# The same fp32 two-block transformer kernel, with its instructions ordered by the framework's finer simulation

## The chip, the cores and the metric

The kernel runs on one core of one Trainium2 chip. The metric is device time in microseconds (us) from launch to end, lower is better. A core has a matrix engine (TensorE, PE in the rows; PEld is its weight load), a vector engine (DVE), an activation engine (ScalarE, ACT), GpSimd (POOL) and SyncE (SP), which here only issues transfers. Each engine runs its own list of instructions in the order in which the program holds them and waits on semaphores for the others.

## The reference

One sequence of 256 tokens, width 1024, all in fp32. First two layers of a mixer with a gate behind it, then one conditioned block with a convolution, a pooling branch and a gated feed-forward:

```python
for i in range(2):                                    # first block
    h = rms_norm(x, pre_norm_g[i])
    y = retention_branch(h, ...) if i == 0 else mla_branch(h, ...)
    x = x + rms_norm(y, post_norm_g[i])
    x = x + (p[i] @ ple_w_proj[i]) * sigmoid(x @ ple_w_gate[i])
mod = silu(c) @ w_ada + b_ada                         # second block
sh1, sc1, g1, sh2, sc2, g2 = split(mod, 6)
h = layer_norm(x) * (1 + sc1) + sh1
# conv branch, pooling branch, two sigmoid gates, all from h @ w_in
mix = (sigmoid(gate_a) * (silu(layer_norm(conv)) @ w_pw) + sigmoid(gate_b) * yb) @ w_out
x = layer_norm(ALPHA * x + g1 * mix)
h = layer_norm(x) * (1 + sc2) + sh2
v, gt = split(causal_dwconv(h @ w_up), 2)
x = layer_norm(ALPHA * x + g2 * ((gelu(gt) * v) @ w_down))
```

The retention branch has 4 heads in two chunks of 128 tokens. The latent attention (MLA) has 16 heads with a causal softmax.

## The kernel before

Activations are kept transposed, 128 features on the partitions and 256 tokens along the row; a `Blk` holds 4 such blocks per tile (named half_N). To be exact in fp32, most products are made from three passes: every operand is split into a high part and a low rest, and `mm` (L232 to L234) issues high times high, high times low and low times high. `mm32` (L238) is the plain fp32 product. The moving side of a pass is 256 columns in most places.

Weights (in_wts) stream in pieces of 128x1024 through SP: `fetch` (L163) loads raw_N, `load` then makes wh_N on ACT (L176) and wl_N on DVE (L177); 6 raw, 5 wh and 5 wl buffers turn round. Activations are split the same way by `split`: ACT writes the high part (L185), DVE the low part (L186):

```python
A.copy(hi, raw)
V.tensor_sub(lo, raw, hi.bitcast(F32))
```

Beside this stream runs the conditioning product `silu(c) @ w_ada`: 48 chunks adach_N of 128x1024, each loaded by SP (L401, two buffers) and reduced on DVE (L408). They are spread through the first two layers by a rate (`mod_rate`).

The order has two makers. The trace of the Python code fixes the order in which instructions are made: `after(us, fn)` and `tick` keep a clock of matmul time and call a prepared step, such as the softmax of a head, when its due time has come. The framework then orders each engine's instructions again before they are fixed, with a simulation of the engines that says which instruction is ready when. The loads of the conditioning chunks (L401) are held in program order among themselves, the rest is free within its data dependences and its buffers.

Sums over features, as the norms need them, are made on PE by a product with a matrix of ones: L336 (`put`) adds one block into a PSUM bank, and the norm can be read only when the last block has been added. L358 does it for a head of the retention. `rms_neg2` and `newton` (L374, L376, L362, L365, L368) make the norm factor from the bank, `ln_stats` the same for a layer norm (L382 to L388).

Four places are spoken of later. `post` ends a layer of the first block:

```python
for k, n in ((0, 1), (1, 1), (2, 2), (4, 2), (6, 1), (7, 1)):
    V.tensor_mul(x1.span(k, n), x1.span(k, n), bc2(nry, n))      # L679
    V.tensor_add(x1.span(k, n), x1.span(k, n), x.span(k, n))     # L680
    split(x1p[0].span(k, n), x1p[1].span(k, n), x1.span(k, n))   # L185, L186
```

and `half_outer` then starts the product with `ple_gate` from the first of these blocks. PE works meanwhile on `ple_proj` (php_N, its result copied by ACT at L724). In the MLA, `mla_scores` makes for each head a row maximum (L874, L875, L877), the exponential on ACT (L879, L880) and the division on DVE (L882, L887), and `mla_turn` transposes the result on PE (L898). `lora` norms the latent (L774, L777, L780, then L185, L186). `modulate` makes the input of the feed-forward (L962, L963, ACT L967, DVE L970 and L974). Behind the convolution, L1162 and a split make the input of `w_pw`.

## Time and profile before

| | |
|---|---|
| time, median of 3 runs | 851.39 us (851.32 to 853.29) |
| the profiled execution: time and span | 853.2 us, 851.4 us |
| PE busy | 834.8 us, 98% of the span |
| DVE busy | 713.2 us, 84% |
| ACT busy | 550.6 us, 65% |
| POOL busy | 9.7 us, 1% |
| weights and other reads from memory | 165.41 MB, 196 GB/s over the span |
| granted TensorE clock, mean | 0.997 |

The span reaches from the first to the last instruction of the core; 1.8 us of the profiled execution lie around it. Busy time of PE is modelled from pipelined matmuls, so that matmuls which follow closely overlap in their rows: the spacing of their starts is what one costs. Times in rows are us from the start of the span.

### The profile page before, as it was taken

The page shows a single profiled execution, that of the slowest core. Times are in us where ns is not written, and L with a number is a line of the kernel's source. Part 1 is how long each engine was busy: PE and PEld are TensorE (multiplying, and loading weights), DVE is VectorE, ACT ScalarE, POOL GpSimd, SP SyncE. Part 2 cuts the span into 40 slices and gives each one's busy share as a digit, 9 for nine tenths or more (in the row PEclk, how much of TensorE's full clock was granted, in tenths as well). Part 3 has the DMA queues.
Part 4 walks back from the last instruction along what each step waited for, and adds up shares of the span by engine and source line. Part 5 has one row for each costly group of instructions (what it writes and reads, how often), then busy time and mean ns, then how long its engine had stood idle before and what let it go on. Part 6 is the DMA issues. An engine that isn't in the chain of part 4 may idle for free.

```text
span 851.4 us, 15952 instructions
## 1 busy us (share of the span) xinstructions
PE 834.8 (98%) x6218; PEld 798.2 (94%) x6218; DVE 713.2 (84%) x1287; ACT 550.6 (65%) x928; POOL 9.7 (1%) x28
## 2 busy tenths in 40 slices
PE   8999999999999999999999999999999999999995
PEld 6989899999999999999999998999999999999885
DVE  6999787898889978699874677899687888889996
ACT  6656555545676686787653757999756576666550
POOL 0000000000000000000000000000000000000001
PEclk9999999999999999999999999999999999999998
DMA  9866566678557647365355354245463365567722
GB/s 334 321 233 235 204 211 245 243 254 293 188 173 243 242 150 237 136 243 179 118 168 174 142 205 156 85 174 177 146 226 134 136 194 179 194 205 253 275 86 74
DMA packets 46634, 167.48 MB, mean 197 GB/s; under 512 B 5216, under 2 KB 5472, under 8 KB 46560
## 3 DMA queue, kind: packets, MB, share of 16 engines
q1 hardware_dynamic: 45936, 164.38, 55.0%
q0 software_dynamic: 624, 2.10, 0.9%
q8 instruction: 48, 0.79, 0.4%
q14 instruction: 26, 0.21, 0.1%
HBM read 165.41 MB, written 1.05 MB: 196 GB/s over the span
## 4 chain that ended last, share of the span: by engine, by line
PE 93%; DVE 4%; DMA 1%; ACT 1%; issue 1%; DVEq 0%; SPq 0%; ACTq 0%
PE ps L233 27%; PE ps L232 26%; PE ps L234 26%; PE ps L238 10%; PE ps L336 1%; PE ps L358 1%; DVE wl L177 1%; PE ps L898 1%; DMA adach<-in_wada 1%; DMA raw<-in_wts 1%; DVE half L679 0%; ACT wh L176 0%; DVE half L680 0%; PE ps L1146 0%; DVE t L1410 0%
## 5 line engine op out<-in xcount | busy, mean ns | idle before, releaser
L232 PE MATMUL ps<-half,wh 128*128 128x256 f32 x1504 | 424.8, 283 | 1.4 <-ACT half L185 1.4
L233 PE MATMUL ps<-half,wh 128*128 128x256 f32 x1504 | 423.6, 282 | 0.6 <-DVE half L186 0.5
L234 PE MATMUL ps<-half,wl 128*128 128x256 f32 x1504 | 422.1, 281 | 0.3 <-DVE wl L177 0.3
L176 ACT CAST wh<-raw 128x1024 fp32r<-128x1024 f32 x233 | 242.9, 1048 | 147.7 <-PE ps L233 94.3
L177 DVE TENSOR_TENSOR wl<-raw,wh 128x1024 fp32r<-128x1024 f32 x233 | 282.3, 1219 | 58.3 <-ACT wh L176 55.8
L233 PEld LDWEIGHTS ps<-half,wh 128*128 128x128 f32 x1504 | 283.3, 188 | 1.9 <-DVE half L186 0.9
L232 PEld LDWEIGHTS ps<-half,wh 128*128 128x128 f32 x1504 | 282.4, 188 | 2.6 <-ACT half L185 2.0
L234 PEld LDWEIGHTS ps<-half,wl 128*128 128x128 f32 x1504 | 283.9, 189 | 0.6 <-DVE wl L177 0.5
L238 PE MATMUL ps<-half,raw 128*128 128x256 f32 (+2 forms) x384 | 84.9, 380 | 0.0
L238 PEld LDWEIGHTS ps<-half,raw 128*128 128x128 f32 x384 | 72.5, 190 | 10.0
L232 PE MATMUL ps<-wh,half 128*128 128x512 f32 (+1 forms) x202 | 72.7, 361 | 0.0
L234 PE MATMUL ps<-wh,half 128*128 128x512 f32 (+1 forms) x202 | 71.0, 351 | 0.0
L233 PE MATMUL ps<-wl,half 128*128 128x512 f32 (+1 forms) x202 | 71.0, 351 | 0.0
L408 DVE CUSTOM_DVE_ANT_0 adach<-adach,siluc 128x1024 f32<-128x1024 f32 x48 | 58.3, 1218 | 11.5 <-DMA adach<-in_wada 11.5
L1063 ACT ACTIVATE t<-apad,vec 128x256 f32<-128x256 f32 x106 | 44.3, 500 | 0.5 <-DVE half L1064 0.5
L233 PEld LDWEIGHTS ps<-wl,half 128*128 128x128 f32 x202 | 38.1, 189 | 5.5 <-DVE wl L177 0.4
L232 PEld LDWEIGHTS ps<-wh,half 128*128 128x128 f32 x202 | 38.0, 188 | 5.5 <-ACT wh L176 0.2
L234 PEld LDWEIGHTS ps<-wh,half 128*128 128x128 f32 x202 | 38.0, 188 | 5.5
L1064 DVE TENSOR_TENSOR half<-half,t 128x512 f32<-128x512 f32 x53 | 36.4, 687 | 3.7 <-ACT t L1063 1.8
L185 ACT CAST half<-t 128x256 fp32r<-128x256 f32 (+1 forms) x47 | 20.3, 452 | 16.9 <-DVE t L1323 10.9
L186 DVE TENSOR_TENSOR half<-t,half 128x256 fp32r<-128x256 f32 (+1 forms) x47 | 21.7, 483 | 3.6 <-ACT half L185 2.7
L1318 ACT ACTIVATE t<-ps,vec 128x256 f32<-128x256 f32 x38 | 21.0, 558 | 2.0 <-PE ps L234 1.2
(277 smaller groups left out, 971.1 us busy)
## 6 DMA issues: line engine op xcount, KB each, us to landing
raw<-in_wts SPq DMA_DIRECT2D x257, 512.0 KB, 4.3
adach<-in_wada SPq DMA_DIRECT2D x48, 512.0 KB, 5.1
half<-in_xT SPq DMA_DIRECT2D x4, 256.0 KB, 6.9
half<-in_rows POOLq DMA_DIRECT2D x2, 512.0 KB, 5.2
out<-t SPq DMA_DIRECT2D x4, 256.0 KB, 2.0
cst<-in_cst SPq DMA_DIRECT2D x1, 928.0 KB, 10.1
raw<-in_wts SPq DMA_DIRECT2D x2, 256.0 KB, 5.1
siluc<-in_cv SPq DMA_DIRECT2D x1, 512.0 KB, 8.1
```

Of the source, the lines that this page charges most:

```text
L176: A.copy(hi, raw)
L177: V.tensor_sub(lo, raw, hi.bitcast(F32))
L185: A.copy(hi, src)
L186: V.tensor_sub(lo, src, hi.bitcast(F32))
L232: T.matmul(ps, l[0], r[0], start=first, stop=False)
L233: T.matmul(ps, l[0], r[1], start=False, stop=False)
L234: T.matmul(ps, l[1], r[0], start=False, stop=last)
L238: T.matmul(ps, w, r, start=first, stop=last)
L408: V.tensor_tensor_reduce(ch, ch, sc, 1.0, 0.0, MUL, ADD, mod[:, n:n + 1])
L1063: A.activation(t[:, b, :], apad[:, i0 + b, k:k + S], AF.Copy, scale=w[b])
L1064: V.tensor_add(acc.pair(i0 // 2), acc.pair(i0 // 2), t)
L1318: A.activation(t[:, b, :], ps[:, b, :], AF.Identity, bias=col("b_dw_f_2", m), scale=w[2])
```

## The change

The context in which the kernel is built is told to order the instructions with the framework's finer simulation of the engines (a timeline) in place of its default one. The kernel's body is the same:

```diff
-    with tile.TileContext(nc) as tc:
+    with tile.TileContext(nc, schedule_with_timeline_sim=True) as tc:
         tile_kernel(tc, order, *aps, out)
```

Both programs hold the same instructions on the same tiles, but for one more table load on ACT; the order on PE, DVE, ACT and SP differs from the start of layer 0 to the end. Three places show how.

**DVE, in `post` of layer 0**, between the norm factor and the first low parts. t1_417 is the norm factor nry, half_413 and half_414 are x1, half_1 and half_2 are x, half_434 is the low part of x1 and wl_451 and wl_457 are low parts of weights that are used later. Before:

```order
L365 TENSOR_TENSOR t1_419_2520<-t1_415_2513,t1_418_2518 128x256
L368 SCALAR_TENSOR_TENSOR t1_417_2517<-t1_419_2520,t1_416_2515 128x256
L679 TENSOR_TENSOR half_413_2508<-half_413_2508,t1_417_2517 128x256 x2
L680 TENSOR_TENSOR half_413_2508<-half_413_2508,half_1_75 128x256 x2
L679 TENSOR_TENSOR half_413_2508<-half_413_2508,t1_417_2517 128x512
L679 TENSOR_TENSOR half_414_2509<-half_414_2509,t1_417_2517 128x512
L680 TENSOR_TENSOR half_413_2508<-half_413_2508,half_1_75 128x512
L186 TENSOR_TENSOR half_434_2600<-half_413_2508,half_432_2598 128x256 x2
```

And now:

```order
L365 TENSOR_TENSOR t1_419_2520<-t1_415_2513,t1_418_2518 128x256
L177 TENSOR_TENSOR wl_451_2723<-raw_449_2720,wh_450_2722 128x1024
L368 SCALAR_TENSOR_TENSOR t1_417_2517<-t1_419_2520,t1_416_2515 128x256
L679 TENSOR_TENSOR half_413_2508<-half_413_2508,t1_417_2517 128x256 x2
L679 TENSOR_TENSOR half_413_2508<-half_413_2508,t1_417_2517 128x512
L679 TENSOR_TENSOR half_414_2509<-half_414_2509,t1_417_2517 128x512
L679 TENSOR_TENSOR half_414_2509<-half_414_2509,t1_417_2517 128x256 x2
L680 TENSOR_TENSOR half_413_2508<-half_413_2508,half_1_75 128x256
L177 TENSOR_TENSOR wl_457_2762<-raw_455_2759,wh_456_2761 128x1024
L680 TENSOR_TENSOR half_413_2508<-half_413_2508,half_1_75 128x256
L680 TENSOR_TENSOR half_413_2508<-half_413_2508,half_1_75 128x512
L680 TENSOR_TENSOR half_414_2509<-half_414_2509,half_2_76 128x512
```

Behind these come two more L680 and then the first L186. All six products L679 and all six sums L680 now stand ahead of the first low part, and two weight pieces among them.

**PE, at the start of the same `post`**: ps_409 is the bank of the norm's sums, t2_412 the last block that goes into it, ps_428 and ps_429 belong to `ple_proj`. Before:

```order
L336 MATMUL ps_409_2485<-t2_411_2502,ones_98 128x256
L232 MATMUL ps_428_2542<-php_391_2363,wh_421_2530 128x256
L233 MATMUL ps_428_2542<-php_392_2364,wh_421_2530 128x256
L336 MATMUL ps_409_2485<-t2_412_2505,ones_98 128x256
L234 MATMUL ps_428_2542<-php_391_2363,wl_422_2531 128x256
```

And now, twelve matmuls of ps_428 and five of ps_429 later than ps_409's other blocks:

```order
L232 MATMUL ps_429_2556<-php_391_2363,wh_421_2530 128x256
L233 MATMUL ps_429_2556<-php_392_2364,wh_421_2530 128x256
L336 MATMUL ps_409_2485<-t2_412_2505,ones_98 128x256
L234 MATMUL ps_429_2556<-php_391_2363,wl_422_2531 128x256
L232 MATMUL ps_429_2556<-php_391_2363,wh_421_2530 128x256
```

The matmul that closes the bank has moved from behind 2 matmuls of `ple_proj` to behind 17.

**DVE, in the MLA near 398 us**: sm_858 is the softmax tile of one head, sm_860 its negated maximum, sm_862 one over its sum. Before:

```order
L877 TENSOR_SCALAR sm_860_4930<-sm_859_4927 128x2
L943 TENSOR_SCALAR ms_6471<-s1_6470 128x8
L1203 TENSOR_TENSOR gs_7666<-s1_6470,vec_77 128x8
L177 TENSOR_TENSOR wl_908_5172<-raw_906_5169,wh_907_5171 128x1024
L882 RECIPROCAL sm_862_4935<-sm_861_4932 128x2
L887 TENSOR_SCALAR sm_858_4926<-sm_858_4926,sm_862_4935 128x128
```

And now:

```order
L177 TENSOR_TENSOR wl_914_5201<-raw_912_5198,wh_913_5200 128x1024
L877 TENSOR_SCALAR sm_860_4930<-sm_859_4927 128x2
L186 TENSOR_TENSOR t2_872_5004<-ps_870_4990,t2_871_5003 128x512
L177 TENSOR_TENSOR wl_920_5224<-raw_918_5221,wh_919_5223 128x1024
L177 TENSOR_TENSOR wl_926_5253<-raw_924_5250,wh_925_5252 128x1024
L747 TENSOR_TENSOR t1_889_5072<-ps_876_5024,cos4_122 128x256
L748 TENSOR_TENSOR t1_888_5067<-t1_888_5067,sin4_123 128x256
L186 TENSOR_TENSOR al_882_5051<-ps_880_5046,ah_881_5050 128x384
L882 RECIPROCAL sm_862_4935<-sm_861_4932 128x2
L749 TENSOR_TENSOR t1_889_5072<-t1_889_5072,t1_888_5067 128x256
L887 TENSOR_SCALAR sm_858_4926<-sm_858_4926,sm_862_4935 128x128
```

The head's last steps now stand behind three later weight pieces (wl_914, wl_920, wl_926) and the turn of the head before it; further up, a reduce of the conditioning product (adach_996) and two splits (t2_869, half_545) have also come ahead of them.

## Rows read from the trace of the kernel before

**Rows 1.** Page, part 1: busy time and share of the span.

```profile
span 851.4 us, 15952 instructions
...
PE 834.8 (98%) x6218; PEld 798.2 (94%) x6218; DVE 713.2 (84%) x1287; ACT 550.6 (65%) x928; POOL 9.7 (1%) x28
```

**Rows 2.** Page, part 4: chain that ended last, shares by engine.

```profile
PE 93%; DVE 4%; DMA 1%; ACT 1%; issue 1%; DVEq 0%; SPq 0%; ACTq 0%
```

**Rows 3.** Waits of PE: total us, times, longest us.

```profile
PE ps L336 <- DVE t L326: 2.5, 1, 2.5
```

**Rows 4.** Page, part 5: busy us, mean ns of one, idle ahead, its releaser.

```profile
L177 DVE TENSOR_TENSOR wl<-raw,wh 128x1024 fp32r<-128x1024 f32 x233 | 282.3, 1219 | 58.3 <-ACT wh L176 55.8
L408 DVE CUSTOM_DVE_ANT_0 adach<-adach,siluc 128x1024 f32<-128x1024 f32 x48 | 58.3, 1218 | 11.5 <-DMA adach<-in_wada 11.5
```

**Rows 5.** Timeline of PE, 215 to 222 us: start, duration, instruction.

```profile
215.43 0.59 PE L336 MATMUL ps<-t,ones 128*128 128x256 f32 x2
...
217.30 0.28 PE L234 MATMUL ps<-php,wl 128*128 128x256 f32 x1
217.41 0.28 PE L232 MATMUL ps<-php,wh 128*128 128x256 f32 x1
...
222.04 0.38 PE L233 MATMUL ps<-half,wh 128*128 128x256 f32 x1 [0.26 <-DVE half L186]
```

**Rows 6.** Timeline of DVE, 216 to 222 us; in brackets idle time ahead, its releaser.

```profile
216.06 0.42 DVE L374 TENSOR_SCALAR t<-ps 128x256 f32<-128x256 f32 x1 [1.25 <-PE ps L336]
...
217.95 0.42 DVE L368 SCALAR_TENSOR_TENSOR t<-t,t 128x256 f32<-128x256 f32 x1
218.41 0.76 DVE L679 TENSOR_TENSOR half<-half,t 128x256 f32<-128x256 f32 x2
219.09 0.76 DVE L680 TENSOR_TENSOR half<-half,half 128x256 f32<-128x256 f32 x2
219.76 1.28 DVE L679 TENSOR_TENSOR half<-half,t 128x512 f32<-128x512 f32 x2
...
221.56 0.75 DVE L186 TENSOR_TENSOR half<-half,half 128x256 fp32r<-128x256 f32 x2
```

**Rows 7.** Timeline of PE and DVE, 481 to 487 us.

```profile
481.53 0.59 PE L336 MATMUL ps<-t,ones 128*128 128x256 f32 x2
...
486.46 0.75 DVE L186 TENSOR_TENSOR half<-half,half 128x256 fp32r<-128x256 f32 x2
...
486.93 0.38 PE L233 MATMUL ps<-half,wh 128*128 128x256 f32 x1 [0.28 <-DVE half L186]
```

**Rows 8.** Timeline of DVE and PE, 387 to 400 us.

```profile
387.15 1.23 DVE L177 TENSOR_TENSOR wl<-raw,wh 128x1024 fp32r<-128x1024 f32 x1 [1.61 <-ACT wh L176]
...
397.98 0.55 DVE L887 TENSOR_SCALAR sm<-sm,sm 128x128 f32<-128x128 f32 x2
...
399.64 0.82 PE L898 MATMUL ps<-ident,sm 128*128 128x128 f32 x6
```

**Rows 9.** Timeline, three other starts of a product: 284, 611 and 671 us.

```profile
284.62 0.62 PE L232 MATMUL ps<-half,wh 128*128 128x256 f32 x3 [1.37 <-ACT half L185]
...
612.15 1.28 ACT L1186 ACT_TABLE_LOAD   x1
...
662.27 0.59 PE L336 MATMUL ps<-t,ones 128*128 128x256 f32 x2
...
671.21 0.75 DVE L974 TENSOR_TENSOR half<-t,half 128x256 fp32r<-128x256 f32 x2
```

**Rows 10.** Stretches: busy us of PE, PEld, DVE, ACT, POOL (instructions), granted clock, DMA share, GB/s.

```profile
24.00:60.00 36.00, 36.00 (x263) 33.98 (x262) 35.70 (x66) 21.56 (x27) 0.00 (x0) 1.00 0.72 275
206.00:213.00 7.00, 5.33 (x46) 5.12 (x44) 7.00 (x9) 6.01 (x11) 0.00 (x0) 1.00 0.80 280
842.00:844.00 2.00, 0.73 (x7) 0.53 (x5) 1.99 (x6) 0.20 (x1) 1.69 (x1) 1.00 0.00 0
846.00:848.00 2.00, 0.00 (x0) 0.00 (x0) 1.93 (x5) 0.00 (x0) 0.00 (x0) 0.71 0.35 131
848.00:850.00 2.00, 0.00 (x0) 0.00 (x0) 0.26 (x1) 0.00 (x0) 0.00 (x0) 0.50 0.70 262
```

## The prediction

> **What bounds the kernel now.** I read the shares of the span first: PE is busy for 834.8 of 851.4 us, DVE for 84% of them and ACT for 65% [rows 1]. The chain that ended last lies on PE for 93% and on DVE for 4% [rows 2]. So PE's list of matmuls is the bound, and another order can change the time only by the stalls in it. I then went through the starts of PE's matmuls. Two that follow each other without a stall are 0.11 to 0.12 us apart (217.30 and 217.41 [rows 5]); what lies above that comes to about 19 us in the whole span, most of it the 5 us of the first loads and two waits, 2.5 us for the sums of a norm (L326) [rows 3] and 1.37 us for the first half of the MLA's latent (L185) [rows 9]. A better order can win 10 to 15 us at most, since the first loads stay.
>
> Next I read how near PE already is to a wait. At the start of `ple_gate0` the first low part L186 starts at 221.56; two of them take 0.75, so the first ends near 221.98, and the matmul that reads it starts at 222.04 [rows 5, 6]. At `ple_gate1` the distance is as small: L186 starts at 486.46, its matmul at 486.93 [rows 7]. Whatever is put ahead of these instructions on DVE comes on to PE at once. DVE isn't free to take it up either: its busy time is 35.70 of 36.00 us in the stretch from 24 to 60 us and 7.00 of 7.00 from 206 to 213 us [rows 10]. Lastly I compared the two orders with these rows.
>
> **What the change does, place by place.** It adds and removes no work but a table load. What moves has a pattern: DVE takes a weight's low part (L177) or a conditioning reduce (L408) that is ready ahead of the step of a serial chain (norm, softmax, split) that isn't, and takes all pieces of one kind before the next kind; PE gets the matmul that closes a sum later. Weight pieces and reduces are dear: 1.22 us each in the group's mean [rows 4], about 1.13 when they follow each other. Where PE waits for the chain, the moved pieces are the price.
>
> *post, layer 0 (222 us).* Before, DVE does L368, two L679, two L680, two long L679, one long L680, then the first L186. From 217.95, the start of L368, to the end of that L186 this takes 4.0 us [rows 6]. Now ahead of L186 stand besides the same pieces two more short L679 (0.76 for a pair that overlaps, 0.67 net), one long L680 (0.6, half of the long pair's 1.28) and two more short L680 (0.67), and two weight pieces (2 x 1.13): 4.2 us. On PE the closing L336 moves from behind 2 matmuls of `ple_proj` to behind 17; 15 matmuls at 0.118 are 1.77, and as the first five of the bank's six matmuls still stand first it lands near 217.0 in place of 215.43 [rows 5]: 1.6 us. Together 5.8; of later stalls of 0.2 and 0.4 us some are taken up, so I put down **5.2**. Below, 3.5 if the norm chain has slack for the closing matmul; above, 6.
>
> *post, layer 1 (486 us).* The same six L679 and six L680 (2.56 us each kind) now stand whole ahead of L186, where two L679, two L680 and one long L679 stood (1.95): 3.2 more, and two weight pieces, 2.3. The closing L336, at 481.53 before [rows 7], moves by 4 matmuls, 0.5. Sum 6.0, less the same absorbed stalls: **5.3**, between 4.6 and 6.
>
> *MLA, one head (398 us).* Before, the two L887 end near 398.5 and the transposes L898 of their tile start at 399.96, within the six that the row at 399.64 groups, so 1.7 us of slack for the first L887, which starts at 397.98 and takes 0.28 [rows 8]. Now ahead of them stand one reduce, three weight pieces, three splits of 512 columns (0.6 each) and L747, L748, L749 and one split of 384 columns (1.5 together): 1.14 + 3.4 + 1.8 + 1.5 = 7.8 us. DVE idles 1.61 us at 387 for a weight's high part [rows 8]; a reduce moves in there, which saves 1.2. PE's own list ahead of the transposes grows by 0.35. 7.8 - 1.2 - 1.7 - 0.35 gives **4.5**, between 3.5 and 5.7 (without the saving).
>
> *Latent of q (284 us).* PE already waits 1.37 us [rows 9]. A reduce and a weight piece (2 x 1.14) and a 512-column step (0.6) come ahead of L780, while another reduce and a weight piece leave the place just before it: **2.5**, between 1 and 2.9.
>
> *Start of w_pw (611 us).* ACT does all four L1162 before the first L185 (1.1 later), and the table load, 1.28 [rows 9], an activation (0.6) and a weight's high part (1.05) before the second; a weight's low part stands ahead of the second L186. PE's filling matmuls cover a part: 1.1 + 0.9 + 0.5 gives **2.3** net, between 0.7 and 3.
>
> *Start of w_up (671 us).* The closing L336 at 662.27 [rows 9] moves behind five fp32 matmuls of 0.44 and its sum's others, to near 666.2. Followed step by step (two norm chains, a copy on ACT ahead of L388, four L963 of 0.6, a weight piece of 1.13, four L970 of 0.33 in a row) the first L974 starts at about 675.3 in place of 671.21 [rows 9]: **4.0**, between 2 and 4.2.
>
> *Layer 0 to 213 us.* Reduces are drawn ahead of the heads' chains; by the moved pieces up to 2.6 us at 60 us, where DVE is full, 1.9 at 137 and 5.6 over 158 to 200. By hand 5. But the 2.5 us wait at 211 [rows 3] is one in which DVE is full [rows 10] because it had waited for conditioning chunks (11.5 us in the whole span [rows 4]). A PE that comes later waits less there, so I take off 2.5: **2.5**, between 0 and 7.6. The loads of those chunks move up on SP by a place or a few; the bytes are the same.
>
> *The rest.* Nine smaller places have bounds of 0.2 to 1.9, and after PE's end the stores of the first half come later by some 0.5: **1.2** in all, between 0 and 6.
>
> Sum: 5.2 + 5.3 + 4.5 + 2.5 + 2.3 + 4.0 + 2.5 + 1.2 = 27.5 us. The profiled execution took 853.2, of which 1.8 lie around the span; its span of 851.4 equals the median of the timed runs, so I add to that: **879 us**, 3.2% slower.
>
> **One thing the sum leaves out.** PE's last matmul ends at 842.73 (0.73 us of work in the stretch from 842) and nothing follows; the granted clock is still 1.00 then, 0.71 on average from 846 to 848 and 0.50 behind [rows 10], so it fell from 2.4 to 1.2 GHz after about 4.1 us without a matmul. The longest wait inside the span, 2.5 us, left it at 1.00 [rows 3, 10]. The waits that I forecast at 222, 486 and perhaps 398 and 671 us are 4 to 6 us long. The Trainium skill (TensorE: Matmul & The Clock Gate, part 1, on the clock gate) states that the clock goes back to the lower level when the engine has been idle and comes back only after sustained work; the trace's end agrees with the fall, and no run here shows the return.
>
> **The rivals.**
> 1. *Slower, and the clock falls too.* Four waits over 4.1 us. If each were followed by as long a stretch at half speed as it took to fall, an estimate from the 4.1 us above, it would cost 2 us each: 27.5 + 8, about 887. For it speaks the end of the trace; against it, that two of the four waits are only just so long, and that a return sooner than assumed would cost less. Chance 25%.
> 2. *Slower by half.* DVE is idle for 16% of the span, and a step that I take for late has been drawn up somewhere earlier: every place comes to its lower end, 3.5 + 4.6 + 3.5 + 1 + 0.7 + 2 is 15.3, 867 us. Chance 18%.
> 3. *No change.* The moved pieces are needed soon anyway, and the waits become earlier ones of the same length. That holds only where PE has slack at the moved step. Against it stands the 0.06 us between L186 and its matmul at 222 and the likeness of 486 [rows 5 to 7]. 851, chance 4%.
> 4. *Faster.* The order draws weight pieces ahead so far that PE's waits on weights, splits and the conditioning chunks at 211 and 284 vanish: 2.5 + 1.4 and some 4 of the small ones, 843 us. It would decide if the pieces ahead of L186 at 222 and 486 were done before the norm factor was ready; at 222 DVE's longest idle there is 1.25 us [rows 6], room for one piece of 1.22 and not for two. Chance 5%.
>
> The forecast of 879 has the remaining 48%, with 872 to 884 as its own range. The range that leaves out no more than 2 in 10 reaches from the lower ends to the fallen clock: 862 to 895. A difference under 0.3% (2.6 us) can't be told from none. Slower by more 91%, within 4%, faster 5%.
>
> **What would show it.** In the profile after, PE should wait about 6 us at `ple_gate0` and `ple_gate1`, released by L186, with two L177 among DVE's rows ahead of it; about 4.5 us at an L898, released by L887; about 4 us at the first L974 of `w_up`; and the 2.5 us at L326 should be smaller. PE's busy time should hardly change while the span grows. I would be wrong in the pieces if those waits are under 2 us, and wrong in all if the sum of PE's waits in the span isn't some 25 us larger. A granted clock below 1.00 behind those waits would speak for the first rival.

## The result: 938 us, 10% slower

The changed kernel takes 938.17 us (median of four runs, 930.26 to 938.93), the kernel before 852.34 beside it. The ratio is 1.097, with a 95% interval of 1.094 to 1.101. The forecast had the sign and the mechanism; the time lies 59 us above it, and outside the range. Three runs of the experiments that took over a third longer than the others of their kernel (1193, 1383 and 1673 us) are left out of every time below.

The page of the changed kernel, parts 1, 4 and 5; they answer to [rows 1, 2, 4]:

```profile
span 936.7 us, 15978 instructions
...
PE 860.4 (92%) x6218; PEld 818.6 (87%) x6218; DVE 718.1 (77%) x1287; ACT 552.8 (59%) x929; POOL 10.2 (1%) x28
...
PE 72%; DVE 14%; DMA 8%; ACT 3%; issue 2%; SPq 0%; DVEq 0%; ACTq 0%
...
L177 DVE TENSOR_TENSOR wl<-raw,wh 128x1024 fp32r<-128x1024 f32 x233 | 283.9, 1221 | 96.6 <-ACT wh L176 95.6
...
L408 DVE CUSTOM_DVE_ANT_0 adach<-adach,siluc 128x1024 f32<-128x1024 f32 x48 | 58.6, 1222 | 27.1 <-DMA adach<-in_wada 27.1
```

DVE and ACT have the same work as before, within 5 us. PE's busy time grew by 26 us with the same 6218 matmuls: they took longer, at a lower clock. The chain that ended last left PE for a fifth of the span more than before and went to DVE and to the transfers of the conditioning chunks. DVE's idle time ahead of weight pieces went from 58 to 97 us, ahead of reduces from 11.5 to 27: an instruction that isn't ready now stands first more often.

The waits of PE in the changed kernel (total us, times, longest us); before, the longest was the one of [rows 3]:

```profile
PE ps L232 <- ACT half L185: 14.5, 4, 5.2
PE ps L358 <- DVE t L297: 12.3, 4, 5.6
PE ps L898 <- DVE sm L887: 9.1, 3, 5.4
PE ps L232 <- ACT half L967: 7.4, 2, 5.5
PE ps L233 <- DVE half L186: 5.3, 3, 2.2
PE ps L1146 <- DVE half L1064: 3.0, 1, 3.0
PE ps L232 <- ACT t L185: 2.8, 1, 2.8
PE ps L233 <- DVE half L974: 2.3, 1, 2.3
```

The spacing of matmul starts gives the account. For each matmul I took the distance to the next one, less the median distance of the same kind in the kernel before; what is left is called excess. Excess over 0.3 us at full clock is a wait: 66.8 us now, 7.1 before. Excess where the granted clock is below 0.99 is the clock: 22.5 us now, none before. The smaller excess went from 10.3 to 7.3. The last matmul starts 13.5 us before the end of the span in place of 8.9. That is 59.7 + 22.5 - 3.0 + 4.6 = 83.8 of the 85.3 us between the two spans; the rest isn't assigned.

Where PE waits (the places with a wait of 1.9 us or more now or before, each place's sum), by the same spacing:

| place, us of the changed kernel | released by | us | forecast, net |
|---|---|---|---|
| heads of layer 0: 44, 64, 147, 201 | L185, then L297 | 3.0 + 4.0 + 5.8 + 2.1 | 2.5 with the next line |
| sums of layer 0: 232 | L326 | 0.3, was 2.7 | in the line above |
| `post`, layer 0: 240, 244 | L185, L186 | 6.0 | 5.2 |
| latent of q: 310 | L185 | 5.4, was 1.5 | 2.5 |
| MLA, two transposes: 433, 436 | L887 | 8.7 | 4.5 |
| `post`, layer 1: 530, 534 | L185, L186 | 6.0 | 5.3 |
| first layer norm: 580, 588 | L967 | 6.1 | in "the rest" |
| convolution: 633 | L1064 | 3.2 | in "the rest" |
| start of `w_pw`: 677, 693 | L185, L186 | 3.7 | 2.3 |
| `w_up`: 717, 734, 746, 749 | L345, L326, L967, L974 | 6.7 | 4.0 |

The end of layer 0 is the case that the prediction worked out at most length. The timeline of DVE in the changed kernel (start, duration, instruction):

```profile
236.27 0.42 DVE L374 TENSOR_SCALAR t<-ps 128x256 f32<-128x256 f32 x1 [1.93 <-PE ps L336]
...
238.18 1.23 DVE L177 TENSOR_TENSOR wl<-raw,wh 128x1024 fp32r<-128x1024 f32 x1
239.32 0.42 DVE L368 SCALAR_TENSOR_TENSOR t<-t,t 128x256 f32<-128x256 f32 x1
239.77 2.63 DVE L679 TENSOR_TENSOR half<-half,t 128x256 f32<-128x256 f32 x6
242.32 0.42 DVE L680 TENSOR_TENSOR half<-half,half 128x256 f32<-128x256 f32 x1
242.66 1.22 DVE L177 TENSOR_TENSOR wl<-raw,wh 128x1024 fp32r<-128x1024 f32 x1
243.80 2.29 DVE L680 TENSOR_TENSOR half<-half,half 128x256 f32<-128x256 f32 x5
246.01 2.29 DVE L186 TENSOR_TENSOR half<-half,half 128x256 fp32r<-128x256 f32 x5
```

And that of PE there, with what follows the wait:

```profile
239.60 0.28 PE L234 MATMUL ps<-php,wl 128*128 128x256 f32 x1
243.29 1.01 PE L232 MATMUL ps<-half,wh 128*128 128x256 f32 x3 [3.41 <-ACT half L185]
246.47 0.58 PE L233 MATMUL ps<-half,wh 128*128 128x256 f32 x1 [2.17 <-DVE half L186]
246.85 0.42 PE L234 MATMUL ps<-half,wl 128*128 128x256 f32 x1
```

From L368 to the end of the first L186 it is about 7.1 us, and 4.0 before [rows 6]. The matmuls behind the wait, of 256 columns, are 0.42 us long in place of 0.28 [rows 5].

The stretches of the same place, and one of an earlier wait (busy us of PE, PEld, DVE, ACT, POOL with instructions; granted clock; DMA share; GB/s):

```profile
47.50:51.00 3.50, 3.48 (x11) 2.82 (x12) 3.50 (x6) 0.00 (x0) 0.00 (x0) 0.62 0.81 307
...
236.00:240.00 4.00, 3.88 (x33) 3.65 (x31) 3.06 (x6) 2.54 (x5) 0.00 (x0) 1.00 0.25 101
240.00:244.00 4.00, 0.71 (x3) 0.71 (x3) 4.00 (x9) 1.78 (x3) 0.00 (x0) 0.86 0.38 131
244.00:248.00 4.00, 1.83 (x9) 1.53 (x9) 4.00 (x10) 2.23 (x5) 0.00 (x0) 0.50 0.35 131
248.00:252.00 4.00, 4.00 (x29) 4.00 (x29) 0.63 (x2) 0.94 (x1) 0.00 (x0) 0.78 0.02 4
```

The clock is 1.00 while PE works, falls to 0.50 (1.2 of 2.4 GHz) in the wait, and is still there when the product with `ple_gate` has begun.

### The profile page after: what moved, and what is told of

The parts are those of the page before. It is cut to its first block, busy times and chain, and to the rows that moved or that the text cites. A ratio compares the mean times of both kernels' runs of the same rounds, so it can differ in the third digit from the quotient of the medians.

```text
span 936.7 us, 15978 instructions
## 1 busy us (share of the span) xinstructions
PE 860.4 (92%) x6218; PEld 818.6 (87%) x6218; DVE 718.1 (77%) x1287; ACT 552.8 (59%) x929; POOL 10.2 (1%) x28
## 4 chain that ended last, share of the span: by engine, by line
PE 72%; DVE 14%; DMA 8%; ACT 3%; issue 2%; SPq 0%; DVEq 0%; ACTq 0%
PE ps L233 21%; PE ps L232 21%; PE ps L234 21%; PE ps L238 7%; DMA adach<-in_wada 6%; DVE wl L177 4%; DVE adach L408 1%; PE ps L336 1%; PE ps L358 1%; DMA raw<-in_wts 1%; ACT wh L176 1%; DMA half<-in_xT 1%; DVE half L680 1%; DVE half L679 1%; PE ps L898 0%
## 5 line engine op out<-in xcount | busy, mean ns | idle before, releaser
L232 PE MATMUL ps<-half,wh 128*128 128x256 f32 x1504 | 428.5, 289 | 21.9 <-ACT half L185 14.5
L233 PE MATMUL ps<-half,wh 128*128 128x256 f32 x1504 | 429.6, 287 | 7.6 <-DVE half L186 5.3
L234 PE MATMUL ps<-half,wl 128*128 128x256 f32 x1504 | 426.6, 285 | 0.0
L176 ACT CAST wh<-raw 128x1024 fp32r<-128x1024 f32 x233 | 243.6, 1049 | 209.9 <-PE ps L233 156.5
L177 DVE TENSOR_TENSOR wl<-raw,wh 128x1024 fp32r<-128x1024 f32 x233 | 283.9, 1221 | 96.6 <-ACT wh L176 95.6
L232 PEld LDWEIGHTS ps<-half,wh 128*128 128x128 f32 x1504 | 288.5, 194 | 24.1 <-ACT half L185 15.5
L233 PEld LDWEIGHTS ps<-half,wh 128*128 128x128 f32 x1504 | 290.2, 193 | 9.2 <-DVE half L186 6.0
L234 PEld LDWEIGHTS ps<-half,wl 128*128 128x128 f32 x1504 | 289.9, 193 | 0.3 <-DVE wl L177 0.2
L238 PE MATMUL ps<-half,raw 128*128 128x256 f32 (+2 forms) x384 | 88.7, 389 | 0.0
L238 PEld LDWEIGHTS ps<-half,raw 128*128 128x128 f32 x384 | 74.0, 194 | 11.5 <-ACT half L973 1.0
L408 DVE CUSTOM_DVE_ANT_0 adach<-adach,siluc 128x1024 f32<-128x1024 f32 x48 | 58.6, 1222 | 27.1 <-DMA adach<-in_wada 27.1
L234 PE MATMUL ps<-wh,half 128*128 128x512 f32 (+1 forms) x202 | 71.8, 358 | 0.0
L234 PEld LDWEIGHTS ps<-wh,half 128*128 128x128 f32 x202 | 38.9, 192 | 5.6
L1064 DVE TENSOR_TENSOR half<-half,t 128x512 f32<-128x512 f32 x53 | 36.3, 687 | 9.0 <-ACT t L1063 6.9
L186 DVE TENSOR_TENSOR half<-t,half 128x256 fp32r<-128x256 f32 (+1 forms) x47 | 21.7, 480 | 6.5 <-ACT half L185 6.5
L185 ACT CAST half<-t 128x256 fp32r<-128x256 f32 (+1 forms) x47 | 20.4, 451 | 8.3 <-DVE t L780 3.8
## 6 DMA issues: line engine op xcount, KB each, us to landing
cst<-in_cst SPq DMA_DIRECT2D x1, 928.0 KB, 11.5
```

What stands on the lines that cost most here:

```text
L185: A.copy(hi, src)
L186: V.tensor_sub(lo, src, hi.bitcast(F32))
L232: T.matmul(ps, l[0], r[0], start=first, stop=False)
L233: T.matmul(ps, l[0], r[1], start=False, stop=False)
L234: T.matmul(ps, l[1], r[0], start=False, stop=last)
L238: T.matmul(ps, w, r, start=first, stop=last)
```

## Experiments

The two kernels differ only in order, so each experiment is a mixture of the two orders. I recorded each engine's list of instructions from the programs of both, edited a list, and held an engine to its list by an edge from each instruction to the next that orders them without a semaphore:

```diff
         tile_kernel(tc, order, *aps, out)
+        pin(tc, nc, ORDER_0)
...
+def pin(tc, nc, text):
...
+    edge = mybir.DependencyInfo(mybir.DependencyClass.NoSync, mybir.DependencyReason.DATA)
+    for a, b in zip(names, names[1:]):
+        tc.add_manual_dep(by[b], a, edge, reason="pin")
```

Where nothing else is said, all five engines are pinned, and the diffs show the first rows by which a list differs from that of its parent kernel. "As before" for a stretch means that the instructions which the kernel before ran in those microseconds stand among themselves in its order. The kernel before ran beside each experiment, with medians of 853.65 to 854.91 us, and the ratios are to it. The four runs of the changed kernel lie up to 9 us apart, so a step of some 5 us between two kernels isn't clear of noise; there the waits in the traces have to decide. No run pins a kernel to its own unchanged list. The nearest is the changed kernel with three rows moved (further down): up to the first of them its waits in the heads are those of the changed kernel within 0.7 us.

### Undoing the ends of the layers, and four other places

In the changed kernel, the stretches of 205 to 240 and 470 to 505 us as before on PE, DVE and ACT; on DVE at the end of layer 0:

```diff
 L365 TENSOR_TENSOR t1_419_2520<-t1_415_2513,t1_418_2518 128x256
-L177 TENSOR_TENSOR wl_451_2723<-raw_449_2720,wh_450_2722 128x1024
 L368 SCALAR_TENSOR_TENSOR t1_417_2517<-t1_419_2520,t1_416_2515 128x256
```

> The changed program with every engine held to its list, except that in two stretches, around the ends of layer 0 and layer 1, PE, DVE and ACT stand as they stood before. Theory A (PE waits where ready pieces stand ahead of a chain's steps, and the clock falls behind the long waits): the two waits of 6.0 us at each layer end go, less the 0.4 to 0.6 us that stood there before, and with them 1.8 and 3.1 us that the matmuls behind them lose at the lower clock: 938 goes to about 922. Theory B (the conditioning chunks hold DVE through their loads): these layer ends hardly take part, 933 or more. Theory C (PE's own list, sums closed later and products opened early, costs the time wherever DVE stands): about half of the 12 us comes back, 930.

Measured 920.98 us, ratio 1.078 [1.075, 1.082]. The two sums of 6.0 us became 0.5 and 0.4. All waits fell from 66.8 to 54.0 us, the excess at the lower clock from 22.5 to 17.4, which makes up the 17 us. The terms that were worked out most closely were right for the waits; the 5 us at the lower clock stood in none of them.

In a second kernel the latent (270 to 300), the MLA (384 to 410), `w_pw` (605 to 618) and `w_up` (650 to 690) were put back as before:

```diff
-L177 TENSOR_TENSOR wl_577_3422<-raw_575_3419,wh_576_3421 128x1024
 L780 SCALAR_TENSOR_TENSOR t1_521_3120<-ps_480_2905,gq_2893,t1_520_3118 128x256
 L780 SCALAR_TENSOR_TENSOR t1_522_3124<-ps_480_2905,gq_2893,t1_520_3118 128x256
+L177 TENSOR_TENSOR wl_577_3422<-raw_575_3419,wh_576_3421 128x1024
```

> The changed program with every engine held to its list, except that PE, DVE and ACT stand as before around four places: the latent norm (wait of 5.4 us), the softmax heads of the MLA near 433 (3.1 and 5.6), the start of w_pw (2.6 and 1.1) and the start of w_up (0.6, 1.5, 2.1 and 2.5). Theory A: 24 us of waits go, less the 1.4 that stood at the latent norm before, and 8 us of lower clock behind them: 938 goes to about 907. Theory B: nothing here hangs on the chunks but the latent norm and the MLA, about 925. If moved pieces only push a wait from one place to the next, it stays above 930.

909.85 us, 1.065 [1.059, 1.072]: 28 us less. The forecast's four terms there come to 13.3; the waits fell by 17.3 us, the excess at the lower clock by 8.5.

Both together, and 505 to 604 us as before besides, which holds the layer norm that the prediction had not seen; the rows are of its sums on PE:

```diff
+L358 MATMUL ps_1124_6509<-t2_1130_6521,ones_98 128x256 x2
...
 L238 MATMUL ps_1120_6493<-half_1116_6477,raw_1123_6505 128x258
...
-L358 MATMUL ps_1124_6509<-t2_1130_6521,ones_98 128x256 x2
```

> The changed program with every engine held to its list, except that PE, DVE and ACT stand as before in the stretches of both earlier experiments (layer ends, latent norm, MLA heads, w_pw, w_up) and also from the first layer norm of the second block to the start of its convolution (waits of 5.6, 0.5 and 3.2 us in the changed program, with 5 us of lower clock behind them). If the places are independent, as theory A has it, the gains add: 938 less 17 and 28 measured and 14 more, 879. If they share a cause further up or a wait moves on, it stays above 890.

879.49 us, which stands on a single run. 17 and 28 from 938 leave 893; the stretch of 505 to 604 is then worth some 14, as expected. As far as one run can show it, the places add up.

### Which engine, which kind of work

The first two rivals to "each place by its own pieces" were the conditioning chunks (theory B of the expectations) and PE's own order (theory C). For the chunks I put the reduces (L408 and the sums behind them) and SP's loads L401 back as before:

```diff
-L408 ISA adach_66_367,mod_116<-adach_66_367,siluc_117 128x1024
-L408 ISA mod_116 128x1
 L453 SCALAR_TENSOR_TENSOR t1_34_194<-t1_32_186,t1_33_192 128x256
 L374 TENSOR_SCALAR t1_36_209<-ps_35_204 128x256
```

> The changed program with every engine held to its list, except that the conditioning reduces on DVE and their loads on SP stand where they stood before. Theory B: DVE's waits on the chunks fall from 27 us towards 11.5, and the waits at the retention heads (17 us between 24 and 235 us, and 4.6 us of lower clock) go with them: about 915. Theory A: the weight pieces stay ahead of the chains, so at most the 5 to 8 us of the reduces themselves come back, 930 to 934.

933.60 us, 1.093 [1.087, 1.100], as theory A has it. The waits of DVE in this kernel (total us, times, longest us):

```profile
DVE wl L177 <- ACT wh L176: 98.4, 102, 4.5
DVE adach L408 <- DMA adach<-in_wada: 12.0, 7, 2.5
```

DVE's idle time ahead of chunks is back at the value of [rows 4], and yet no more than some 5 of 85 us came back, which isn't clear of noise. PE's waits in the heads shrank to 1.7, 2.8 and 2.8 us, but 3.9 and 1.8 appeared at 221 and 229. So most of the loss stands without the chunks being moved.

The converse, the kernel before with its reduces and loads of chunks where the change has them:

```diff
 L408 ISA mod_116 128x1
+L408 ISA adach_67_369,mod_116<-adach_67_369,siluc_117 128x1024
+L408 ISA mod_116 128x1
 L362 TENSOR_TENSOR t1_39_214<-t1_37_211 128x256
```

> The program of before with every engine held to its list, except that the conditioning reduces and their loads stand where the change puts them. Theory B: the waits at the heads appear here too, 852 goes to about 868 to 872. Theory A: reduces alone cost what stands ahead of a chain with no slack, up to 5 us: 852 to 857.

896.05 us, 1.049 [1.042, 1.056]. Both theories missed this by far. The waits of DVE for chunks in this kernel come to more than in the whole changed kernel, 27.1:

```profile
DVE adach L408 <- DMA adach<-in_wada: 33.4, 17, 5.6
```

One part of an order, moved alone, is worth 42 us in one company and 5 in another. That the weight pieces which stand ahead of the reduces in the change, and give the loads time, now stand behind them would explain the sign; it wasn't tried.

For PE's order I took the finer simulation and pinned PE alone to the order of before; DVE, ACT and SP were then ordered by the simulation:

```diff
-    with tile.TileContext(nc) as tc:
+    with tile.TileContext(nc, schedule_with_timeline_sim=True) as tc:
         tile_kernel(tc, order, *aps, out)
+        pin(tc, nc, ORDER_0)
```

> The finer simulation with PE alone held to its list of before; DVE, ACT and SP are ordered by the simulation. Theory C (PE's own list): most of the 85 us come back, 855 to 870. Theory A: DVE and ACT still put ready pieces ahead of the chains, only the sums that close late on PE come back, 890 to 910.

929.01 us, 1.087 [1.081, 1.093], higher than both expected. The waits of PE in this kernel:

```profile
PE ps L232 <- ACT t L185: 17.7, 4, 7.6
PE ps L232 <- ACT half L185: 13.0, 5, 3.6
```

With PE's list of before the waits are as long in sum (64.5 us), at other places. So PE's list alone doesn't bring the time back, and theory C falls. What PE's list is worth isn't shown, though: with PE pinned, the simulation gave DVE and ACT lists that are neither those of before nor those of the change, as their rows in the trace show. The same kernel with DVE and ACT pinned to before, and PE and SP ordered by the simulation:

```diff
         tile_kernel(tc, order, *aps, out)
+        pin(tc, nc, ORDER_0)
+        pin(tc, nc, ORDER_1)
```

> The finer simulation with DVE and ACT held to their lists of before; PE and SP are ordered by the simulation. With PE alone held, 929 was measured, so the cost should sit on DVE and ACT. Theory A: 855 to 870, what is left being sums that PE closes late. Theory C: PE's own order costs as much again, above 890.

883.97 us, 1.036 [1.032, 1.039], between the two. Waits are 27.8 us, the clock 8.0. With DVE and ACT in their order of before some 54 of the 85 us are gone. The other 30 aren't the price of the change's order on PE and SP: PE's list in this kernel is a third one, which differs from that of before in more rows than the change's does. How the 85 us divide between the engines isn't shown.

### The first 212 us

The largest gap in the table is at the top. The kernel before, with its first 212 us in the order of the change on all engines:

```diff
 L442 TENSOR_SCALAR t1_31_183<-t1_30_181 128x256
-L177 TENSOR_TENSOR wl_47_247<-raw_45_244,wh_46_246 128x1024
+L177 TENSOR_TENSOR wl_53_272<-raw_51_269,wh_52_271 128x1024
 L443 TENSOR_SCALAR t1_31_183<-t1_31_183 128x256
```

> The program of before with every engine held to its list, except that the first 212 us, the projections and the heads of layer 0, stand on all engines as the change puts them. Prediction's term for this stretch: 2.5 us, 856. By the waits in the changed program's trace: 17 us of waits and 5 us at the lower clock, less the 2.7 that stood at the sums of layer 0, 872.

873.81 us, 1.023 [1.019, 1.026]: about 20 us, as the trace said, where the term of the sum was 2.5. The timeline of DVE in this kernel, ahead of one closing L358 (the whole of its wait is 6.7 us):

```profile
144.97 1.23 DVE L177 TENSOR_TENSOR wl<-raw,wh 128x1024 fp32r<-128x1024 f32 x1 [1.09 <-ACT wh L176]
148.49 1.23 DVE L408 CUSTOM_DVE_ANT_0 adach<-adach,siluc 128x1024 f32<-128x1024 f32 x1 [2.29 <-DMA adach<-in_wada]
...
149.64 1.22 DVE L177 TENSOR_TENSOR wl<-raw,wh 128x1024 fp32r<-128x1024 f32 x1
150.78 1.22 DVE L408 CUSTOM_DVE_ANT_0 adach<-adach,siluc 128x1024 f32<-128x1024 f32 x1
...
154.09 1.22 DVE L408 CUSTOM_DVE_ANT_0 adach<-adach,siluc 128x1024 f32<-128x1024 f32 x1
...
155.24 0.42 DVE L297 TENSOR_TENSOR t<-t 128x256 f32<-128x256 f32 x1
```

L297 is what PE waits for. Ahead of it stand a weight piece that waits for its high part (L176, which in turn waits for a buffer that PE's L234 frees), a reduce that waits for its chunk, and three more pieces. Idle time is 3.4 us of this, the pieces are the larger part. To tell the two kinds apart, the same kernel with the reduces and SP's loads as before:

```diff
-L408 ISA adach_66_367,mod_116<-adach_66_367,siluc_117 128x1024
-L408 ISA mod_116 128x1
 L453 SCALAR_TENSOR_TENSOR t1_34_194<-t1_32_186,t1_33_192 128x256
```

> The kernel before with its first 212 us in the order of the change on PE, DVE and ACT, but the reduces of the conditioning chunks and SP's loads left where they stood before. The same edit with them moved took 21.5 us, with PE waits of 2.78, 3.99, 6.67 and 2.37. Theory A (the moved reduces, and their waits for chunks, stand in the chain ahead of the closing sums; the weight pieces and the dependent matmuls alone cost little): the waits of 3.99 and 6.67 fall to under 2 each, the time is 853 to 861. Theory B (weight pieces ahead of the chain, which need a slot that TensorE frees, and closing sums further back on TensorE do it; the chunks only fill the gaps): waits of 3 or more stay at both places, the time is 864 to 874.

869.62 us, 1.017 [1.012, 1.021]: some 4 or 5 of 20 us less, with intervals that overlap. By time it is theory B; by the two waits it lies between, as they fell from 4.0 and 6.7 to 2.85 each. What they lost came up further on: at 219, 224 and 298 us PE waits 2.2, 3.2 and 3.1, where the kernel with the reduces moved had 0.3 or less, and 1.5. The stretch of 20 to 212 us in the kernel before, in this one with the heads of the change, and with the chunks put back:

```profile
20.00:212.00 192.00, 191.33 (x1460) 183.93 (x1458) 171.59 (x271) 109.30 (x138) 1.21 (x2) 1.00 0.70 250
```

```profile
20.00:212.00 192.00, 176.39 (x1271) 167.79 (x1270) 161.04 (x257) 97.17 (x118) 1.21 (x2) 0.96 0.66 233
```

```profile
20.00:212.00 192.00, 185.09 (x1379) 177.47 (x1378) 163.79 (x257) 102.03 (x122) 1.22 (x2) 0.98 0.65 227
```

Before, DVE does 171.6 us of work in 192: it is 89% full. In the mixtures it does 10.6 and 7.8 us less in the same time. In the first 215 us DVE's waits for high parts of weights went from 8.1 to 10.7 and 15.2 us, those for chunks from 8.8 to 11.2 and 6.0. By these sums about half of the missing work is idle time behind pieces drawn ahead whose input isn't there; for the rest I take steps that wait for the late PE, which isn't shown. My reading is that DVE doesn't get it back in a stretch this full, and that what is late comes to PE here or a little later.

### The clock

In the changed kernel I put 208 matmuls of a matrix of ones by itself into 14 of PE's waits, into a bank that is overwritten by what follows; the results don't change (n is 3 to 26, by place; the line of `fill` is shortened):

```diff
-        ps = [bank2() for _ in range(2)]
+        ps = [bank2() for _ in range(2)]; fill(ps[0][:, 0, :])
...
+fill = lambda ps: [T.matmul(ps[:, :P], ones, ones, start=True, stop=True) for _ in range(n)]
```

> The changed program with every engine held to its list, and 208 idle matmuls of ones, 0.21 us each, put on PE into 14 of its waits, each wait filled to within 0.4 us; they add work that nothing reads. If the lower clock is what follows a wait without matmuls, the 22 us that are lost at it nearly all come back and the waits stay: 916 to 920. If the clock falls for another reason, or the waits are given back elsewhere, 938 or more.

924.81 us, 1.082 [1.079, 1.086]. Its clock over the span:

```profile
core 0: 922.4 us, clock 0.990
```

The mean clock of the changed kernel is 0.958. The excess at the lower clock fell from 22.5 to 4.3 us. Of these 18 us, 13 came back, 5 fewer than expected at the least; the smaller excess rose by 2.6, as some fills are longer than the wait that they stand in. With nothing else moved, keeping the clock up is worth some 13 of the 85 us.

### The terms at the end of a layer

The changed kernel with three rows moved: in layer 1 the two weight pieces behind the first two L186, in layer 0 the closing L336 back behind two matmuls of `ple_proj`:

```diff
+L336 MATMUL ps_409_2485<-t2_412_2505,ones_98 128x256
 L234 MATMUL ps_428_2542<-php_391_2363,wl_422_2531 128x256
...
-L336 MATMUL ps_409_2485<-t2_412_2505,ones_98 128x256
 L234 MATMUL ps_429_2556<-php_391_2363,wl_422_2531 128x256
```

> The changed program with every engine held to its list but for three instructions: at the end of layer 0 the matmul that closes the norm's sum stands behind 2 matmuls of ple_proj again, and at the end of layer 1 the two weight pieces stand behind the first two low parts. By the terms of the prediction the waits at ple_gate0 (3.6 and 2.5 us) come to 4.4 together in place of 6.0, those at ple_gate1 to 3.8. If the wait is set by something else, a weight's high part or the load of a piece, they stay at 6.0. The time itself moves by 4 to 8 us, 930 to 934.

934.27 us, 1.094 [1.089, 1.099]. Layer 1: 2.42 + 1.34 = 3.8 us in place of 6.0, so two pieces are worth 2.3 as put down. Layer 0: 6.2, no gain. The timeline of ACT in this kernel shows why:

```profile
236.00 0.29 ACT L312 ACTIVATE sm<-t,eps_r 128x1 f32<-128x1 f32 x1
238.06 0.59 ACT L724 COPY half<-ps 128x512 f32<-128x512 f32 x1 [1.77 <-PE ps L234]
238.55 0.48 ACT L376 ACTIVATE t<-ps,eps_r 128x256 f32<-128x256 f32 x1
```

The norm's L376 stands behind L724, the copy of the first `ple_proj` bank, and that waits until PE has finished the bank. In the changed kernel the closing sum came after that bank, so nothing showed. Then also L376 ahead of L724, and layer 0's two pieces behind its first two L186:

```diff
+L376 ACTIVATE t1_416_2515<-ps_409_2485,eps_r_110 128x256
 L724 COPY half_426_2540<-ps_428_2542 128x512
-L376 ACTIVATE t1_416_2515<-ps_409_2485,eps_r_110 128x256
```

> The changed kernel with the layer ends taken apart: in both layers the two weight pieces behind the first two L186; in layer 0 also the closing L336 back behind two matmuls of the projection, and ScalarE's L376 ahead of the bank copy L724. The run without the last of these and without layer 0's two pieces waited 3.50 and 2.73 there and took 934.3. Theory A (the prediction's terms are right, and L724 held up what the closing matmul gained): layer 0's waits fall from 6.2 to 1.5 to 2.2, the time to 929 to 931. Theory B (something else sets layer 0's chain): over 3.5 left, the time 932 to 935.

929.24 us, 1.086 [1.081, 1.090]; the time is theory A's. Layer 0 waits 2.0 us for L185, and 1.0 more for a weight piece that now comes too late, together above A's bound and under B's. L376 runs 1.3 us behind L312, in place of 2.6.

### Can the idea be used

Two kernels tried it. In the kernel before, the last four chunks of layer 0 reduced later, to shorten the wait at 211 us [rows 3], and in the latent a reduce and a weight piece moved behind L186:

```diff
-L408 ISA adach_381_2273,mod_116<-adach_381_2273,siluc_117 128x1024
...
 L177 TENSOR_TENSOR wl_448_2693<-raw_446_2690,wh_447_2692 128x1024
+L408 ISA adach_381_2273,mod_116<-adach_381_2273,siluc_117 128x1024
```

> The program of before with every engine held to its list but for a few places in which theory A is turned round, with ready pieces put behind the chain: the last four conditioning chunks of layer 0 are loaded and reduced after the sums at 211 us, and at the latent norm one reduce and one weight piece stand behind L186. Theory A: the waits of 2.7 and 1.5 us go, about 4 us, 0.5% faster. If DVE or the loads bound that stretch, they come back at the next wait and nothing changes.

857.47 us (median of eleven), 1.004 [1.003, 1.006]: no gain, and if anything slightly slower. The waits of PE in this kernel:

```profile
PE ps L234 <- DVE wl L177: 3.4, 2, 3.0
```

The 2.5 us at L326 went to 0.3, and 1.3 and 1.1 us came up at 219 and 243 behind the same reduces; the weight piece of the latent was moved too far.

The changed kernel with its first 240 us and every place above as before; left in the new order are 300 to 384, 410 to 470 and what follows 690 us:

```diff
 L177 TENSOR_TENSOR wl_29_175<-raw_4_86,wh_28_174 128x1024
-L189 SCALAR_TENSOR_TENSOR half_13_133<-half_2_76,vec_77,half_11_131 128x256 x2
+L189 SCALAR_TENSOR_TENSOR half_13_133<-half_2_76,vec_77,half_11_131 128x256 x3
```

> The changed program with every engine held to its list, except that the first 240 us, too, stand as before on all engines, beside all the places of the earlier experiments (all but 300 to 384, 410 to 470 and the last 160 us of the program of before). If the places found are the whole, what is left is 4 to 5 us at the end of the program: 857 to 860. If much of the loss lies outside of them, 870 or more.

862.09 us, 1.010 [1.006, 1.014]. The heads (some 20 us), the ends of the layers, the four places, and 505 to 604 make up 76 of the 85 us. Nothing here beats the kernel before.

## Why the prediction was right in kind and wrong in size

**Right.** The mechanism, and the ends of the layers. The prediction put 6 us at `ple_gate0` and `ple_gate1`, released by L186 with two L177 ahead of it; 6.0 and 6.0 came, the first matmul held by ACT's L185 and the second by L186. The wait at L326 of [rows 3] all but went, from 2.7 to 0.3 by the spacing. The list of waits of the changed kernel has another one at L326, but that belongs to a norm ahead of `w_up`, 500 us further on:

```profile
735.57 2.43 PE L336 MATMUL ps<-t,ones 128*128 128x256 f32 x10 [1.37 <-DVE t L326]
```

In the parts, two weight pieces are 2.3 us, as said.

**The step that failed most: "Layer 0 to 213 us", 2.5.** That stretch alone, put into the kernel before, measured some 20. The working had 5 us by hand and took 2.5 off, because a late PE waits less at 211. That absorption did come. Wrong was the 5, and the upper end of 7.6. By hand there were 2.6 us at 60, 1.9 at 137 and 5.6 over 158 to 200; measured are 4.0 at 64, 5.8 at 147 and 2.1 at 201, and 3.0 at 44, where none was put down. The working counted the durations of the pieces moved ahead. It put most of the loss at 158 to 200, where 2.1 came, and it had no term for DVE's standing still behind the pieces (3.4 us ahead of the wait of 6.7 shown above), although [rows 10] had DVE at 35.7 of 36 us in one stretch; and with the lower clock behind the waits this part came to 20.

**The clock was left out of the sum.** Rival 1 had four waits with 2 us each behind them, 8 in all, from the one wait that the trace of before had of such a length, the end. In the changed kernel eleven stretches inside the span run at 1.2 GHz, each behind a wait. The matmuls in them lose 22.5 us, and PE's busy time, which "should hardly change", grew by 26. The rival had the right mechanism and, with 887, was still 51 us short: the clock fell at eleven places and not four, and the waits themselves were too small in the sum. The return, which no run of before showed, is in the stretch of 248 to 252 us, whose mean is 0.78. The fall after a wait and the return after work agree with what the Trainium skill (TensorE: Matmul & The Clock Gate, part 1, on the clock gate) states.

**Places that were not seen, "the rest", 1.2.** At 580 us PE waits 5.6 for the first layer norm of the second block. The timeline of PE in the changed kernel ahead of it, with the wait's end:

```profile
565.68 9.09 PE L238 MATMUL ps<-half,raw 128*128 128x258 f32 x41
574.60 1.03 PE L358 MATMUL ps<-t,ones 128*128 128x256 f32 x4
...
585.41 0.80 PE L232 MATMUL ps<-half,wh 128*128 128x256 f32 x2 [5.45 <-ACT half L967]
```

And in the kernel before:

```profile
509.63 6.26 PE L238 MATMUL ps<-half,raw 128*128 128x258 f32 x28
515.78 1.10 PE L358 MATMUL ps<-t,ones 128*128 128x256 f32 x4
...
519.31 8.00 PE L238 MATMUL ps<-half,raw 128*128 128x258 f32 x36
```

The sums L358 now close behind 56 fp32 products (41 in this window, 56 in the chain) in place of 28, and the fill of 36 products that hid the norm is used up: only 8 are left behind the sums. 28 x 0.22 is 6.1 us. My comparison looked at DVE's and ACT's work ahead of the waiting matmul, and not at PE's own work ahead of the sum further up. With 0.5 more at 588 and the convolution's 3.2, "the rest" is 9 us of waits.

**Terms that were too small in size.** MLA 8.7 for 4.5: two transposes wait, the second one 5.6 us, and I worked out one head. Latent 3.9 net for 2.5, `w_pw` 3.7 for 2.3, `w_up` 6.7 for 4.0, each above its upper bound: the pieces drawn ahead at `w_up` act in four waits and not in one. Layer 0's `post` was right in sum, and its 1.6 us for the closing L336 true only together with L724 on ACT: moved alone it gave nothing.

**The end.** 0.5 forecast, 4.6 measured: the last norm of the first half now ends behind the last matmul. The last matmul of the changed kernel, and the first sum on POOL behind the norm of the first half:

```profile
923.22 0.28 PE L234 MATMUL ps<-wh,half 128*128 128x256 f32 x1
...
927.80 3.41 POOL L1408 TENSOR_TENSOR t<-t,half 128x512 f32<-128x512 f32 x2 [31.23 <-DVE t L1407]
```

In the kernel before, that sum starts at 842.31, just ahead of the last matmul at 842.45.

**Sum.** 27.5 forecast; the first 232 us +10 (12.5 of waits for 2.5), the MLA, the latent, `w_pw` and `w_up` +10, the unseen places +9, the clock +22.5, the end +4, the ends of the layers +1.5: 84.5 of the 85 us, all rounded. One reading of the prediction was off without touching this: of the 19 us that lie above the spacing in the kernel before, the first loads and the two waits are 8.9, not most.

**Open.** Why the reduces moved alone cost 42 us, and how the loss divides between the orders of PE, DVE, ACT and SP, isn't settled: the mixtures run into waits that the change itself doesn't have, and where the simulation ordered the engines that weren't pinned, its orders aren't those of the change. No run speaks for the rivals of no change or of a gain.

## What to carry to other kernels

An engine that keeps to its list and is nearly full, like DVE here, must not meet an instruction whose input or buffer isn't there: ask of each piece drawn ahead what it waits for, and not only how long it takes. When you compare two orders by hand, follow each wait back through every engine, the waiting engine's own list too, to the sum that starts the chain. And on a kernel that keeps the matrix engine at full clock, price each new wait twice: for itself, and for the matmuls at the lower clock behind it.

## What was not expected of the hardware

The lower clock came behind waits shorter than the 4.1 us of the end [rows 10]: after 3.0 us at 44 us the granted clock was 0.62 in the stretch of 47.5 to 51. Even the wait of 2.6 us at 677 was followed by a stretch at 0.50, though the one of 2.7 us at 211 in the kernel before left the clock at 1.00, so that the length of a wait alone doesn't tell:

```profile
680.00:683.00 3.00, 2.80 (x13) 2.80 (x14) 0.43 (x1) 2.97 (x5) 0.00 (x0) 0.50 0.02 5
```

And filled waits kept the clock at 0.99 with matmuls that do no useful work.
